# One expert's first 128 rows computed from a shorter list, between the steps of the last routing; expert weights loaded three chunks a block

## The chip, the cores and the metric

The kernel runs on one core of a Trainium2 chip. The metric is the device time of one execution in microseconds (us); a run's figure is the median of its executions.

## What is computed

One layer: an RMSNorm with modulation, a bidirectional HGRN2 mixer over 1024 latent and 256 context tokens, a residual, then a second norm and a mixture of experts (16 experts of width 256, two per token, chosen within the best group of four), a residual and a final RMSNorm. All data is float32. The part that matters here:

```python
s = jax.nn.sigmoid(h @ router_w)                    # h: (1024, 1024), 16 experts
sel = (s + router_b).reshape(n, 4, 4)
top_v, top_i = lax.top_k(sel, 2)
best = jnp.argmax(jnp.sum(top_v, axis=-1), axis=-1)
ids = best[:, None] * 4 + jnp.take_along_axis(top_i, best[:, None, None], axis=1)[:, 0]
w = jnp.take_along_axis(s, ids, axis=1); w = w / jnp.sum(w, axis=-1, keepdims=True)
for e in range(16):
    a = jax.nn.silu(h @ w_gate[e]) * (h @ w_up[e])
    y = y + combine[:, e:e + 1] * (a @ w_down[e])
```

With the given inputs expert 0 gets 140 of the 1024 tokens: 103 from the first six blocks of 128 tokens and 37 from the last two. The experts' counts are 140, 121, 148, 99, 307, 289, 122, 94, 81, 84, 119, 52, 47, 104, 143 and 98.

## The kernel before, in words

The order of instructions on every engine is the order of the code (a manual schedule), with hardware semaphores between engines. The change lies in the last third.

**The output projection and the routing** (loop `for b in range(2, NLB)` and what follows it). For each block b of 128 tokens TensorE (PE) multiplies the mixer's output with the output weights (`yo`, L904 to L906), VectorE (DVE) adds the residual (`x_evac`, `x_add`, L1012 and L1017) and forms the normed row h (`x_norm`, L1045), which SyncE (SP) stores to `h2_d` in DRAM. One block behind follow the router: `x_flip` transposes the block on PE (L1058; ScalarE (ACT) copies it, L1059), `partial` multiplies it with the router's weights (L1069), `logits` finishes that (L1076), `choose` picks the experts on DVE (L1089 to L1120), and `rank` counts on PE (L1127 to L1131, tile `pos`) which place in its expert's list each token takes, on top of `cum`, the counts of all blocks before. `enlist` (L1157) and `enlist_weights` with `enlist_rest` (L1172, L1178) write the token numbers and the weights, by one-hot matmuls that accumulate over all blocks, into the two PSUM tables `tab[0]` and `tab[1]`. Column q = 8 e + j of a table is the j-th list of 128 rows of expert e.

After the last block the tables are copied to `tidx` (L1317) and `wtab`, the counts to `cnt`. A place in a list with no token holds a number that is out of bounds, and the indirect DMAs skip it.

**Loading the experts' weights.** SP loads them in chunks of 512 KB (`load_chunk`, L962 and L965) into slots `ew`. Thirteen chunks have slots before the expert loop: experts 0 and 1's gate and up (0 to 7), expert 0's down (8, 9) and part of expert 2's. From b = 2 on, two chunks follow each block, and the thirteenth follows the loop. Each chunk is split into a high and a low float32r part: the high one on ACT (`split_hi`, L985), the low one on DVE or GpSimd (POOL) (`split_lo`, L990).

**The expert loop.** For expert e and list j: POOL gathers the 128 rows from `h2_d` (`fetch`, L1181), PE transposes them (`flip`, L1367; ACT and DVE split them, L1374 and L1375), then 24 matmuls (`gate_up`, L1381 to L1383), the activation (`act`, L1387 and L1388), two transposes (`flip_a`), 12 matmuls (`down`, L1407 to L1409), the weighting (L1410), and POOL adds the rows to `x1_d` in DRAM with an accumulating indirect DMA (`add_rows`, L1396). `finish` starts the next expert's `flip` before this expert's `down`. An expert with more than 128 rows takes a second pass (the branch `more`), one with more than 256 a third; `deep`, skipped here, does more. Ahead of the loop POOL gathers the first list of expert 0 (`gbuf[0]`) and clears two buffers (L1363), and after the branch for `deep` it gathers expert 0's second list if there is one (`fetch_if(0, 1)`), clears a buffer (L1509) and gathers expert 1's first list, then expert 2's.

## Time and profile before

| | us |
|---|---|
| median of 3 runs (lowest, highest) | 1112.74 (1108.35, 1114.17) |
| the profiled execution's own time | 1110.9 |
| span of its trace | 1108.6 |
| PE busy | 1040.0 (94%) |
| DVE busy | 695.7 (63%) |
| ACT busy | 506.8 (46%) |
| POOL busy | 260.6 (24%) |

The profile is of one execution; the times in it count from the span's start. A busy PE counts overlapping matmuls, so the spacing of their starts is what one costs. The profile's first part gives busy times by engine, its second the span in slices; the windows give the same for any stretch, with the granted clock of TensorE as a fraction of its full 2.4 GHz (0.50 is 1.2 GHz). The timelines list instructions in order with the idle time ahead of each.

### The profile page before, as it was taken

How to read it: one execution, taken by the hardware profiler on the slowest of the kernel's cores; microseconds unless marked ns; L12 is line 12 of the kernel's file. 1: busy time of each engine (PE TensorE's matmuls, PEld its weight loads, DVE VectorE, ACT ScalarE, POOL GpSimd, SP SyncE). 2: the span in 40 equal slices, each digit the busy share in tenths (PEclk: the TensorE clock that was granted, in tenths of full speed). 3: DMA queues.
4: the chain of work that ended last, by engine and by line, in shares of the span. 5: the costliest groups of instructions: out<-in, count | busy, mean ns of one | idle time of the engine just before them, and what ended most of it. 6: DMA issues, size and time to landing. Idle time of an engine off the chain costs nothing.

```text
span 1108.6 us, 16315 instructions
## 1 busy us (share of the span) xinstructions
PE 1040.0 (94%) x5847; PEld 858.9 (77%) x5847; DVE 695.7 (63%) x1339; ACT 506.8 (46%) x852; POOL 260.6 (24%) x208
## 2 busy tenths in 40 slices
PE   4988999999999999999999999989995999999986
PEld 2566888888888888889889897777774878877764
DVE  3686541146558476584745648777787665588856
ACT  4676231226436273462825635432224553377544
POOL 1353020000000000000000001531114765487834
PEclk9999999999999999999999999999995999999998
DMA  8704443421333214240120301445647997699947
GB/s 298 273 10 143 142 133 110 134 73 57 101 95 105 82 48 134 62 130 22 39 62 20 100 20 53 168 171 178 218 144 256 299 290 242 178 321 322 321 106 303
DMA packets 126225, 165.30 MB, mean 149 GB/s; under 512 B 10099, under 2 KB 93188, under 8 KB 126114
## 3 DMA queue, kind: packets, MB, share of 16 engines
q1 hardware_dynamic: 119634, 147.50, 39.8%
q0 software_dynamic: 6480, 16.39, 6.3%
q8 instruction: 61, 1.00, 0.4%
q14 instruction: 50, 0.41, 0.1%
HBM read 138.02 MB, written 33.05 MB: 154 GB/s over the span
## 4 chain that ended last, share of the span: by engine, by line
PE 64%; DMA 17%; DVE 11%; issue 3%; ACT 2%; POOL 1%; SPq 1%; POOLq 0%; DVEq 0%; ACTq 0%
PE proj L122 10%; PE proj L124 10%; PE proj L123 10%; DMA gb<-h_d,tidx 6%; PE proj L748 3%; PE proj L747 3%; PE proj L749 3%; PE sc L527 3%; DMA x_d<-y,ci 3%; PE o L553 2%; DMA ew<-in_moe_w_gate_dram 2%; PE kv L499 2%; DMA ew<-in_moe_w_up_dram 2%; DMA x_d<-y,tidx 2%; PE yo L904 2%
## 5 line engine op out<-in xcount | busy, mean ns | idle before, releaser
L122 PE MATMUL proj<-HL,whi 128*128 128x512 f32 x512 | 205.7, 402 | 1.6 <-POOL wlo L92 1.1
L123 PE MATMUL proj<-HL,whi 128*128 128x512 f32 x512 | 201.4, 393 | 6.1 <-POOL HL L298 5.5
L124 PE MATMUL proj<-HL,wlo 128*128 128x512 f32 x512 | 200.9, 392 | 1.2 <-DVE wlo L92 1.2
L560 POOL TENSOR_TENSOR oss<-oss,mhalf 128x4 f32<-128x4 f32 x16 | 16.2, 1010 | 472.1 <-DVE oss L559 472.1
L123 PEld LDWEIGHTS proj<-HL,whi 128*128 128x128 f32 x512 | 97.0, 189 | 28.0 <-POOL HL L298 8.4
L122 PEld LDWEIGHTS proj<-HL,whi 128*128 128x128 f32 x512 | 96.9, 189 | 24.1 <-issue 3.0
L124 PEld LDWEIGHTS proj<-HL,wlo 128*128 128x128 f32 x512 | 96.7, 189 | 22.1 <-DVE wlo L92 1.6
L145 ACT ACTIVATE s<-proj 128x512 f32<-128x512 f32 (+1 forms) x46 | 24.0, 523 | 182.9 <-PE proj L124 182.8
L631 DVE SCALAR_TENSOR_TENSOR macc<-mw,sc,macc 128x512 f32<-128x512 f32 x56 | 42.8, 765 | 45.2 <-DMA mw<-in_w_mod_dram 45.2
L503 DVE SCALAR_TENSOR_TENSOR w<-w,ge,kv 128x128 f32<-128x128 f32 x112 | 37.5, 347 | 40.1 <-PE kv L499 37.3
L748 PE MATMUL proj<-vl,HL 128*128 128x512 f32 x128 | 50.3, 393 | 1.2 <-DVE vl L726 1.0
L747 PE MATMUL proj<-vh,HL 128*128 128x512 f32 x128 | 50.1, 391 | 0.0
L92 DVE TENSOR_TENSOR wlo<-ws,whi 128x1024 fp32r<-128x1024 f32 (+1 forms) x31 | 37.8, 1220 | 19.4 <-ACT whi L91 19.4
L749 PE MATMUL proj<-vh,HL 128*128 128x512 f32 x128 | 49.8, 389 | 0.0
L756 ACT COPY vs<-proj 128x512 f32<-128x512 f32 x20 | 11.8, 588 | 78.5 <-PE proj L749 70.0
L1375 DVE TENSOR_TENSOR tl<-mt,th 128x512 fp32r<-128x512 f32 x46 | 29.7, 686 | 27.8 <-ACT th L1374 27.7
L553 PE MATMUL o<-w,qi 128*128 128x128 f32 x256 | 41.3, 284 | 3.6 <-DVE qi L541 1.7
L390 DVE TENSOR_TENSOR_SCAN s<-smask,s 128x1024 f32<-128x1024 bf16 x16 | 36.5, 2282 | 10.2 <-ACT s L383 10.2
L990 POOL TENSOR_TENSOR dn0l<-ew,dn0h 128x1024 fp32r<-128x1024 f32 x16 | 38.3, 2418 | 6.2 <-ACT dn0h L985 6.1
L553 PEld LDWEIGHTS o<-w,qi 128*128 128x128 f32 x256 | 35.1, 198 | 4.6 <-DVE qi L541 2.8
L1387 ACT ACTIVATE ab<-gu 128x256 f32<-128x256 f32 x23 | 8.8, 384 | 65.1 <-PE gu L1383 65.1
L558 ACT ACTIVATE jk<-o 128x128 bf16<-128x128 f32 x64 | 17.8, 277 | 43.9 <-PE o L553 42.3
(467 smaller groups left out, 2739.3 us busy)
## 6 DMA issues: line engine op xcount, KB each, us to landing
ws<-in_hg_w_in_dram SPq DMA_DIRECT2D x36, 512.0 KB, 4.6
mw<-in_w_mod_dram SPq DMA_DIRECT2D x64, 256.0 KB, 2.9
ew<-in_moe_w_gate_dram SPq DMA_DIRECT2D x64, 256.0 KB, 6.5
ew<-in_moe_w_up_dram SPq DMA_DIRECT2D x64, 256.0 KB, 7.0
ew<-in_moe_w_down_dram SPq DMA_DIRECT2D x32, 512.0 KB, 9.2
v_d<-vs SPq DMA_DIRECT2D x20, 256.0 KB, 2.2
v<-v_d SPq DMA_DIRECT2D x8, 640.0 KB, 5.9
xt<-in_x_dram SPq DMA_DIRECT2D x8, 512.0 KB, 5.4
```

What stands on the lines that cost most here:

```text
L92: (G if "l" in pool else V).tensor_sub(lo[:, o, :], ws[:, o, :], hi[:, o, :].bitcast(F32))
L122: PE.matmul(ps[:, :n], hi[:, k, :], Hhi, start=(k == 0), stop=False)
L123: PE.matmul(ps[:, :n], hi[:, k, :], Hlo, start=False, stop=False)
L124: PE.matmul(ps[:, :n], lo[:, k, :], Hhi, start=False, stop=(k == KT - 1))
L390: V.tensor_tensor_scan(L[:, rev], smask[:, 0:T], L[:, rev], 0.0, OP.mult, OP.add)
L503: V.scalar_tensor_tensor(w[:, n + 1, :], w[:, n, :], ge[:, 16 + n:17 + n], p[:, i, :], op0=OP.mult, op1=OP.add)
L553: PE.matmul(p[:, i, :], qi[d][:, i, :, :].rearrange("p j t -> p (j t)"), hd["w", d][:, lat_block(d, l), :], start=False, stop=(d == 1))
L631: V.scalar_tensor_tensor(mod_rest[r], w, sc[:, 0, k:k + 1], mod_rest[r], op0=OP.mult, op1=OP.add)
L747: PE.matmul(ps, hi, wh, start=(k == 0), stop=False)
L748: PE.matmul(ps, hi, wl, start=False, stop=False)
L749: PE.matmul(ps, lo, wh, start=False, stop=(k == KT - 1))
L990: eng.tensor_sub(gl, staged.pop(i), gh.bitcast(F32))
```

## The change

The tables are read once more, early. In the pass of the last block (b = 7), when blocks 0 to 5 are enlisted, `early_list` reads expert 0's first list from `tab[0]` and its weights from `tab[1]` (tiles `eix`, `ewt`), gathers these rows into `early["x"]`, and raises expert 0's count in `cum` to at least 128, so that expert 0's tokens of blocks 6 and 7 go to its second list. `early_flip` transposes the rows, `early_gate` multiplies one of eight row groups with the weights as loaded (plain float32, no split), and its eight calls are strewn between the steps of the last routing. The activation, two transposes and four float32 matmuls of the down projection follow, and `add_rows(ey, eix)` adds the result, all ahead of `deep`. In the expert loop expert 0 then begins with list 1 (`base(0)` is 1), held in `gbuf[0]`; its list 0 is never gathered again. Weights are loaded three chunks a block from b = 2 on, none after the loop. SP is added to the engines that get the branch hint of `deep`.

```diff
+    eix = mp.tile([128, 1], I32, name="eix")
+    ewt = mp.tile([128, 1], F32, name="ewt")
...
+    def gather_rows(dst, ix, n=T):
+        G.indirect_dma_start(out=dst, out_offset=None, in_=h2_d[0:n, :],
+                             in_offset=bass.IndirectOffsetOnAxis(ap=ix, axis=0), bounds_check=n - 1, oob_is_err=False)
...
+    early = {}
+    def early_list():
+        PE.matmul(pos[:, GB, :], onb, cum, start=True, stop=True, skip_group_check=True)
+        V.tensor_scalar(eix, tab[0][:, 0:1], pio, None, op0=OP.add)
+        early["x"] = cp.tile([128, D], F32, name="xr", bufs=2)
+        gather_rows(early["x"], eix, T - 256)
+        S.copy(ewt, tab[1][:, 0:1])
+        short = ct([1], "short")
+        V.tensor_scalar(short[0:1], pos[0:1, GB, 0:1], -1.0, float(CAP), op0=OP.mult, op1=OP.add)
+        V.scalar_tensor_tensor(cum[0:1, 0:1], short[0:1], 0.0, cum[0:1, 0:1], op0=OP.max, op1=OP.add)
+    def early_flip():
+        t_ = early["t"] = cp.tile([128, D], F32, name="x1", tag="x1", bufs=2).rearrange("p (k n) -> p k n", k=KT)
+        for hf in range(2):
+            p = yop.tile([128, 512], F32, name="yo", bufs=3).rearrange("p (k n) -> p k n", k=4)
+            for k in range(4):
+                PE.transpose(p[:, k, :], early["x"][:, (hf * 4 + k) * 128:(hf * 4 + k + 1) * 128], ident)
+            S.copy(t_[:, hf * 4:hf * 4 + 4, :], p)
+        early["p"] = yop.tile([128, 512], F32, name="yo", bufs=3)
+    def early_gate(*ks):
+        for k in ks:
+            PE.matmul(early["p"], early["t"][:, k, :], staged[k // 2][:, k % 2 * 512:k % 2 * 512 + 512], start=(k == 0),
+                      stop=(k == KT - 1))
...
         if b == NLB - 1:
+            early_list()
             choose(NLB - 2)
...
-        for i in range(2 * b - 4, 2 * b - 2):
+        for i in range(3 * b - 6, 3 * b - 3):
             if i < NC0:
                 load_chunk(i)
-    for i in range(2 * NLB - 4, NC0):
-        load_chunk(i)
     x_norm(NLB - 2)
     partial(NLB - 1, low)
+    early_flip()
     x_flip(NLB - 1, 1)
     enlist(NLB - 2)
+    early_gate(0)
     partial(NLB - 1, high)
+    early_gate(1)
     x_norm(NLB - 1, (0,))
     logits(NLB - 1)
     enlist_rest()
     x_norm(NLB - 1, (1,))
+    early_gate(2, 3, 4)
...
     choose(NLB - 1)
     rank(NLB - 1)
+    early_gate(5, 6)
     enlist(NLB - 1)
...
-    gather(gbuf[0], 0)
+    gather(gbuf[0], 1)
...
     enlist_weights(NLB - 1)
+    early_gate(7)
     enlist_rest()
+    ebuf = dn_tiles(1, F32)[1].rearrange("p k n -> p (k n)")
+    ea, eat, ey = ebuf[:, 0:DE], ebuf[:, DE:2 * DE].rearrange("p (k n) -> p k n", k=2), ebuf[:, D:2 * D]
+    S.activation(ea, early["p"][:, 0:DE], AF.Silu)
+    V.tensor_tensor(ea, ea, early["p"][:, DE:], OP.mult)
+    eap = yop.tile([128, 512], F32, name="yo", bufs=3)[:, 0:DE].rearrange("p (k n) -> p k n", k=2)
+    for k in range(2):
+        PE.transpose(eap[:, k, :], ea[:, k * 128:(k + 1) * 128], ident)
+    S.copy(eat, eap)
...
+    def base(e):
+        return 1 if e == 0 else 0
...
+    for hf in range(2):
+        o = slice(hf * 512, (hf + 1) * 512)
+        for k in range(2):
+            PE.matmul(dpp[hf], eat[:, k, :], staged[8 + k][:, o], start=(k == 0), stop=(k == 1))
+        V.scalar_tensor_tensor(ey[:, o], dpp[hf], ewt, g2r[:, o], op0=OP.mult, op1=OP.mult)
+    add_rows(ey, eix)
     deep()
...
-    fetch_if(0, 1)
     fetch_if(0, 2)
...
-    flip(0, 0)
+    flip(0, base(0))
```

In the loop `gate_up`, `act`, `finish` and `before` take `base(e)` where they had 0.

PE, from the last block's first half of the router (`partial`, low) to the branch of `deep`. Before (`ctr` is the router's work, `tab` the two tables, `pos` the counts):

```order
L1069 MATMUL ctr<-x1T,rwp 32x128 x4
L1058 MATMUL ctr<-ident,x_7036 128x128 x4
L1157 MATMUL tab_6119<-qoh,roh 128x128 x2
L1069 MATMUL ctr<-x1T,rwp 32x128 x4
L1076 MATMUL ctr<-four,lt 128x16
L1178 MATMUL tab_6120<-qow,roh 128x128 x2
...
L1131 MATMUL pos<-msk,tri 128x16
L1157 MATMUL tab_6119<-qoh,roh 128x128 x2
...
L1178 MATMUL tab_6120<-qow,roh 128x128 x2
L1472 TENSOR_LOAD cnt
```

And changed (`yo<-ident,xr` is `early_flip`, `yo<-ew` is `early_gate`, `dp<-ew` is the early down projection; four of these last, two shown):

```order
L1071 MATMUL ctr<-x1T,rwp 32x128 x4
L1208 MATMUL yo<-ident,xr 128x128 x8
L1060 MATMUL ctr<-ident,x_7044 128x128 x4
L1159 MATMUL tab_6121<-qoh,roh 128x128 x2
L1214 MATMUL yo<-ew_6049,x_7185 128x512
L1071 MATMUL ctr<-x1T,rwp 32x128 x4
L1214 MATMUL yo<-ew_6049,x_7185 128x512
L1078 MATMUL ctr<-four,lt 128x16
L1180 MATMUL tab_6122<-qow,roh 128x128 x2
L1214 MATMUL yo<-ew_6050,x_7185 128x512 x2
L1214 MATMUL yo<-ew_6051,x_7185 128x512
...
L1133 MATMUL pos<-msk,tri 128x16
```

Further down two gate matmuls stand between `pos` and `tab[0]`, one between `tab[0]` and `tab[1]`, and the two transposes and four down matmuls between `tab[1]` and the first `TENSOR_LOAD`.

POOL, from the gather of expert 0's rows to that of expert 1's. Before:

```order
L1181 DMA gb_6045<-h_d,tidx 128x1024
L1363 MEMSET gb_7309 128x1024
L1363 MEMSET gb_7311 128x1024
L1472 TENSOR_LOAD cnt
...
L1181 DMA gb_7309<-h_d,tidx 128x1024
...
L1509 MEMSET gb_7307 128x1024
L1181 DMA gb_7307<-h_d,tidx 128x1024
```

And changed:

```order
L1183 DMA gb_6047<-h_d,tidx 128x1024
L1413 MEMSET gb_7352 128x1024
L1413 MEMSET gb_7354 128x1024
L1446 DMA x_d<-dn1l,eix 1024x1024
L1522 TENSOR_LOAD cnt
...
L1564 MEMSET gb_7350 128x1024
L1183 DMA gb_7350<-h_d,tidx 128x1024
```

The accumulating DMA of the early rows now stands ahead of the branch and of expert 1's gather (`gb_7350`), and the gather of expert 0's second list (before, into `gb_7309`) is gone.

SP, the end of the last two blocks. Before and changed:

```order
L1026 DMA x_d<-x_7036 128x1024
L962 DMA ew_6057<-in_moe_w_gate_dram 128x2x256
L962 DMA ew_6057<-in_moe_w_up_dram 128x2x256
...
L1049 DMA h_d<-h_6864 128x1024
L1047 DMA h_d<-h_7042 128x512 x2
```

```order
L964 DMA ew_6061<-in_moe_w_gate_dram 128x2x256
L964 DMA ew_6061<-in_moe_w_up_dram 128x2x256
L1028 DMA x_d<-x_7044 128x1024
L1051 DMA h_d<-h_6872 128x1024
L1049 DMA h_d<-h_7050 128x512 x2
```

The last three chunks (six DMAs) no longer stand between the last block's x1 and its h rows.

## Rows read from the trace of the kernel before

**Rows 1.** Windows by stage: us, busy time per engine, PEclk, DMA share, GB/s.

```profile
840.00:850.00 10.00, 2.05 (x7) 1.64 (x7) 5.75 (x22) 3.81 (x6) 5.52 (x4) 0.50 0.58 199
...
871.00:980.00 109.00, 108.61 (x524) 88.37 (x523) 68.15 (x108) 57.40 (x85) 64.54 (x35) 1.00 0.82 243
...
980.00:1060.00 80.00, 76.07 (x359) 59.64 (x358) 68.23 (x92) 56.28 (x77) 62.12 (x31) 1.00 1.00 319
```

**Rows 2.** Timeline of PE, 832 to 853 us: start, length, instruction [idle before <-releaser].

```profile
832.45 1.08 PE L1058 MATMUL ctr<-ident,x 128*128 128x128 f32 x4 [2.55 <-DVE x L1017]
...
835.28 0.61 PE L1076 MATMUL ctr<-four,lt 128*128 128x16 f32 x2 [0.41 <-DVE lt L1072]
...
839.06 0.17 PE L1131 MATMUL pos<-msk,tri 128*128 128x16 bf16 x1 [2.10 <-DVE msk L1116]
...
841.26 0.79 PE L1157 MATMUL tab<-qoh,roh 128*128 128x128 f32 x2 [2.03 <-DVE qoh L1147]
...
844.11 1.22 PE L1178 MATMUL tab<-qow,roh 128*128 128x128 f32 x4 [2.02 <-DVE qow L1172]
...
851.19 1.94 PE L1367 MATMUL mt<-ident,gb 128*128 128x128 f32 x8 [5.86 <-DMA gb<-h_d,tidx]
...
853.01 0.80 PE L1381 MATMUL gu<-gu0h,th 128*128 128x512 f32 x1
```

**Rows 3.** Windows around TensorE's clock, columns as in rows 1.

```profile
831.50:832.00 0.50, 0.00 (x0) 0.00 (x0) 0.47 (x2) 0.00 (x0) 0.00 (x0) 0.80 0.00 0
...
855.50:856.00 0.50, 0.50 (x4) 0.37 (x3) 0.50 (x2) 0.50 (x2) 0.50 (x1) 0.80 0.98 342
```

**Rows 4.** Timeline of PE, 859 to 877 us: expert 0's second pass, expert 1.

```profile
859.92 1.03 PE L1367 MATMUL mt<-ident,gb 128*128 128x128 f32 x8
...
867.21 1.04 PE L1367 MATMUL mt<-ident,gb 128*128 128x128 f32 x8
...
871.02 0.48 PE L1381 MATMUL gu<-gu4h,th 128*128 128x512 f32 x1
...
876.70 1.04 PE L1367 MATMUL mt<-ident,gb 128*128 128x128 f32 x8
```

**Rows 5.** Timeline of DVE, 828 to 872 us.

```profile
828.18 0.16 DVE L1138 SCALAR_TENSOR_TENSOR rm<-rt,row 128x2 f32<-128x2 f32 x1
...
842.09 0.35 DVE L1317 TENSOR_SCALAR tidx<-tab,pio 128x128 int32<-128x128 f32 x1 [0.55 <-PE pos L1315]
...
843.71 0.60 DVE L1172 TENSOR_SCALAR qow<-iop,rq,wr 128x128 f32<-128x128 f32 x2
...
871.08 0.75 DVE L1410 SCALAR_TENSOR_TENSOR y<-dp,wtab,g2r 128x512 f32<-128x512 f32 x1 [0.47 <-PE dp L1409]
```

**Rows 6.** Timeline of ACT, 817 to 872 us.

```profile
817.90 1.08 ACT L1059 COPY x1T<-ctr 128x512 f32<-128x512 f32 x2 [0.86 <-PE ctr L1058]
...
833.57 0.59 ACT L1059 COPY x1T<-ctr 128x512 f32<-128x512 f32 x1 [0.45 <-PE ctr L1058]
...
871.30 0.37 ACT L1392 CAST ax0h<-sp 128x256 fp32r<-128x256 f32 x1 [2.25 <-PE sp L1367]
```

**Rows 7.** Timeline of POOL, 844 to 873 us.

```profile
844.79 2.98 POOL L1181 DMA_INDIRECT gb<-h_d,tidx  x1 [3.41 <-DVE qow L1172]
...
852.60 1.00 POOL L1181 DMA_INDIRECT gb<-h_d,tidx  x1 [2.96 <-issue]
...
854.85 1.63 POOL L1181 DMA_INDIRECT gb<-h_d,tidx  x1 [0.27 <-POOL gb L1509]
...
872.12 1.64 POOL L1396 DMA_INDIRECT x_d<-y,tidx  x1 [6.32 <-DMA gb<-h_d,tidx]
```

**Rows 8.** Tile view of the gathers that POOL starts at 854.85, 857.73, 859.89.

```profile
DMA to landing us min/median/max: 6.0/7.7/9.3
```

**Rows 9.** Chain of waits near the end: start, length, what.

```profile
1085.01 1.72 PE mt L1561 x4
```

**Rows 10.** Chain of waits, last store of the routed rows.

```profile
837.21 6.57 DMA h_d<-h
```

More of the change, by code (lines that the diff above doesn't have):

```diff
@@ L1178, in enlist_rest @@
             PE.matmul(tab[1], r_.bitcast(F32), q_, start=first, stop=last, skip_group_check=True)
+    def gather_rows(dst, ix, n=T):
+        G.indirect_dma_start(out=dst, out_offset=None, in_=h2_d[0:n, :],
+                             in_offset=bass.IndirectOffsetOnAxis(ap=ix, axis=0), bounds_check=n - 1, oob_is_err=False)
     def gather(dst, q):
-        G.indirect_dma_start(out=dst, out_offset=None, in_=h2_d,
-                             in_offset=bass.IndirectOffsetOnAxis(ap=tidx[:, q:q + 1], axis=0),
-                             bounds_check=T - 1, oob_is_err=False)
+        gather_rows(dst, tidx[:, q:q + 1])
+    early = {}
[20 more added lines that the diff above has]
+                      stop=(k == KT - 1))
     alls, low, high = range(KT), range(KT // 2), range(KT // 2, KT)
@@ L1310 @@
     tc.mark_branch_hint_location("deep", "LikelyTaken", [mybir.EngineType.PE, mybir.EngineType.Activation,
-                                                         mybir.EngineType.Pool, mybir.EngineType.DVE])
+                                                         mybir.EngineType.Pool, mybir.EngineType.DVE,
+                                                         mybir.EngineType.SP])
     choose(NLB - 1)
     rank(NLB - 1)
+    early_gate(5, 6)
     enlist(NLB - 1)
@@ L1339 @@
     NJ, NS = T // CAP, 3
+    def base(e):
+        return 1 if e == 0 else 0
     def rows_of(e, j):
-        return gbuf[(e % 3, 3 + e % 2, 5)[j]]
+        return gbuf[0 if j == base(e) == 1 else (e % 3, 3 + e % 2, 5)[j]]
     def fetch(e, j):
@@ L1446, in finish @@
             return
-        with tc.If(nval[e] > (j + 1) * CAP, label=f"more{e}" if j == 0 else None) as cmp:
+        with tc.If(nval[e] > (j + 1) * CAP, label=f"more{e}" if j == base(e) else None) as cmp:
             flip(e, j + 1)
@@ L1457, in before @@
     def before(e, j):
-        if j == 0:
+        if j == base(e):
             if e < NE - 1:
@@ L1530 @@
             split_chunk(i + 1, V)
-        tc.mark_branch_hint_location(f"more{e}", nval[e] > CAP, [mybir.EngineType.PE])
-        gate_up(e, 0)
+        tc.mark_branch_hint_location(f"more{e}", nval[e] > (base(e) + 1) * CAP, [mybir.EngineType.PE])
+        gate_up(e, base(e))
         if e + 1 < NE:
@@ L1539 @@
             fetch(e + 3, 0)
-        act(0)
+        act(base(e))
         if e + 1 < NE:
@@ L1546 @@
                 load_chunk(q + NCH)
-        finish(e, 0)
+        finish(e, base(e))
         fetch_if(e + 1, 2)
```

## The prediction

> **What bounds the kernel now.** I read the windows by stage first, then the timelines of PE and POOL over the change, then the chain of waits for single prices. From 871 to 980 us PE is busy 108.6 of 109 us, and from 980 to 1060 it is busy 95% beside a DMA share of 1.00 [rows 1]: the expert loop runs at PE's pace, its end almost so, with the weights' loads filling the DMA engines. What expert 1 gains or loses at its start is therefore carried to the end of the kernel. The stretch before is different. From 840 to 850 us PE is busy 2.05 of 10 us [rows 1]: the last routing is a chain of small steps on DVE with PE waiting 2.55, 0.41, 2.10, 2.03 and 2.02 us between them, and then 5.86 us for the gather of expert 0's rows [rows 2]. TensorE's granted clock falls to its lower level, 1.2 GHz, just before 832 us, in the first of these waits, and is back at 2.4 GHz only after 855.5 us, some 4.5 us after PE started to work without pause at 851.19 [rows 2, 3].
>
> **What is removed.** Expert 0 has 140 rows and takes two passes. The second starts at 859.92 and expert 1's 24 matmuls at 871.02, 11.1 us later [rows 4]. In the changed kernel the loop has one pass for expert 0, so this stretch shrinks to the flip of expert 1's rows: at most 1.8 us at the low clock (851.19 to 853.01 [rows 2]). **If nothing else waits, 9.3 us go.**
>
> **What is added ahead of the end of the routing.** I follow it to the table `tidx`, which DVE starts at 842.09 and ends at 842.44 [rows 5].
> - DVE: three small instructions in `early_list`. A small one costs 0.16 us, spaced by about 0.2 [rows 5]; DVE works here without a gap, so 0.65 us.
> - ACT: the two copies of `early_flip`, 1.08 us for two [rows 6], stand ahead of the copy that the last router step needs; ACT was idle for 0.45 us there [rows 6], so 0.6 us.
> - PE, `early_flip`: eight transposes, 1.03 us [rows 4], in PE's idle 2.55 us [rows 2]. They wait for the early gather. That cannot be issued before DVE has `eix`, by the order of DVE about 824.5; with 1 us of issue and 6.4 us from start to use (844.79 to 851.19 [rows 2, 7]) it is there at about 832, a little before PE's next step is due at 833.1. I take nothing; if it comes late, PE stands, in order, and every us late is a us of the chain.
> - PE, `early_gate`: a float32 matmul of 128x512 is two records; four took 1.72 us at the end of the kernel, at the high clock [rows 9], so 0.86 us each, or 1.72 at the low clock. Gate 0 lies mostly beside ACT's copies (0.3 us seen), gate 1 covers a wait of 0.41 us (0.45 us seen). Gates 2 to 4 with `tab[1]`'s matmuls (0.6 at the high clock) take 3.2 us where PE's next step was 3.17 us away (835.89 to 839.06), gates 5 and 6 1.7 us where PE waited 2.03, and gate 7 is inside 2.02 us [rows 2]: hidden. All this at the high clock. PE now works almost without pause from 832 on, so I expect the clock back by about 837, as it came back after 4.5 us of work before; the chain's own matmuls that ran at the low clock gain some tenths.
>
> Sum to `tidx`: 0.65 + 0.6 + 0.3 + 0.45 = **2.0 us later**, 844.4.
>
> The three chunks that SP issued ahead of the last h rows are loaded earlier, where there is room. The last store of h took 6.57 us, to 843.78 [rows 10], and set the time of the first gather; now it is early and `tidx` is what counts. That buys 1.3 us of the 2.0 for expert 0's gather, which is in time anyway, as the next part shows.
>
> **The new wait.** The early rows' result is added to `x1_d` by a DMA that POOL issues ahead of the branch and of the gather for expert 1, and POOL works in order. So that gather now waits for the early down projection, which has no cover:
> - DVE's `qow` ends at 844.31 [rows 5], now 846.3. Behind it: `tab[1]`'s matmuls 0.6 us (half of 1.22 at the low clock [rows 2]), two transposes 0.25 (a quarter of 1.03 [rows 4]), ACT's copy of 128x256 0.4 [rows 6], four float32 matmuls 3.44 [rows 9], the weighting 0.75 [rows 5], hand-overs 0.2: 851.9.
> - POOL's add: 0.3 to start, 1.64 [rows 7], so 853.9.
> - Branch and counter reads: POOL's gap of 2.96 us ahead of the gather at 852.60; then a clear and a gap, 1.25 us from the end of that gather to the start of expert 1's at 854.85 [rows 7]. So expert 1's gather starts at 858.1, against 854.85 now.
> - Its landing: 6.0, 7.7 and 9.3 us for this gather and the two behind it [rows 8]. I take 7.0, near its own value with a little for the add's traffic: **865.1**.
>
> Before, expert 1's rows were needed at 867.21 [rows 4] and had landed by 861. Now PE ends expert 0's single pass at about 860 (its gather at 851.8, 1.8 us of flip, 5.6 to 6.9 of matmuls) and stands still for some 5 us. In that idle time the clock falls, as it did at 832 [rows 3]. Flip 1.8 us and two transposes 0.25: expert 1 starts at 867.2, with 1.2 us to come for its first matmuls at the low clock (853.01 to 859.92 took 6.9 us, 871.02 to 876.70 5.7 [rows 2, 4]). That is 868.4 against 871.02: **2.6 us faster**, so 6.7 of the 9.3 us are lost to the new wait. The profiled execution took 1110.9, which makes 1108.3; it lies 1.8 below the median, so for the median 1112.7 - 2.6 = **1110.1**.
>
> The bounds: the landing between 6.0 and 9.3 us moves this by -1.0 and +2.3, the sum to `tidx` between 0.65 (DVE alone) and 3.0 by -1.35 and +1.0. So 2.6 lies between 5.0 faster and 0.7 slower. By the Trainium skill (DMA: Bandwidth & Descriptors, Anatomy of one DMA) a DMA from GpSimd takes about 2.0 us plus its bytes at 436 GB/s, 3.2 us for these 512 KB as an estimate; by that the gather would land 3.8 us earlier and the gain would be 6.4 us. The rows here show twice that under load.
>
> **The rivals.**
> - *The whole pass is won* (over 5.5 us). The gather for expert 1 would have to land by 860, 5 us before my figure, so that PE passes from expert 0 to expert 1 without a pause: 9.3 us, 1103.4. For it: of the 2.96 us on POOL I do not know what is left when the branch's code is ready, and the landing may be short. Against it: on POOL the add stands in front in the changed order, and 4.0 us of float32 matmuls and transposes must be done first. Chance 0.23, with all that lies between.
> - *The clock never falls.* If the transposes and gates keep TensorE at 2.4 GHz from 832 on, the chain's matmuls take half (0.8 us less over the 1.08 and 0.61 us of flip and `logits` [rows 2]), `tidx` is 1.2 us late, not 2.0, and the gain is 3.4 us: 1109.3. For it: the first idle stretch is broken up. Against it: the transposes wait for the early gather, so PE is idle for 2 us first, about as long as before the fall. Chance 0.15. The Trainium skill (TensorE: Matmul & The Clock Gate, HAM oscillation) has it that waits make the array's clock fall and unbroken work keeps it up; by that rule filling the waits is worth something, and the trace agrees that the clock fell in the first of them.
> - *The gates clog the routing* (slower). It decides if the clock is not back when gates 2 to 4 start, near 839. At the low clock gate 0 adds 0.8 and gate 1 0.85 us more, gates 2 to 4 with `tab[1]` take 6.4 us against 3.2, and gates 5 and 6 3.4 against 2.03: `tidx` is about 8 us late. The float32 matmuls behind cost another 4.3. Expert 1's gather starts near 868.7 and expert 1, by the same steps, at 879.0: 8.0 us slower, 1120.7. For it: PE has pauses at the chain's waits. Against it: from 834 on these are short. Chance 0.1.
> - *The change does not do what it says.* If early rows were still computed in the loop, no pass would go; the loop's code starts expert 0 at list 1, so I give this nothing.
>
> **How the numbers follow.** About 0.5% (5.6 us) is what a measurement of this kernel can tell from no change. My forecast, 1107.8 to 1113.4, has 0.52 and the clock's rival 0.15; both lie within it. Over 5.6 us faster: 0.23 from the first rival and 0.02 from the early ends of the forecast, 0.25. Slower by over 5.6: 0.1 from the clogged routing. That leaves 0.65 for the same. The range takes in the forecast with its bounds, most of the first rival and the start of the third: 1102.5 to 1118.0.
>
> **What would show it.** Right: 22 passes through the experts' activation, not 23; POOL's add of the early rows near 852, its gather for expert 1 near 858; PE idle some 5 us before expert 1's flip, that wait ended by a gather, the clock low again after it; `tidx` about 2 us later. Wrong: expert 1 starting before 862 or after 873, the early transposes held up past 834 by their gather, or gates at 1.72 us after 840.

## The result: 6 to 7 us slower, and the profile after

| | before | after |
|---|---|---|
| median of 16 runs each, same chip (us) | 1111.55 | 1118.57 |
| ratio, with its 95% interval | 1 | 1.0056 [1.0033, 1.0078] |
| the profiled execution's own time | 1110.9 | 1121.3 |
| span of its trace | 1108.6 | 1119.5 |

The change costs 7.0 us by the medians. The execution that was profiled shows 10.4 us, for single executions of the changed kernel lie between 1113.57 and 1123.06; the two traces say where. Expert 0 does run one pass less, and PE is busy for longer all the same:

```profile
PE 1046.6 (93%) x5836; PEld 859.7 (77%) x5836; DVE 691.7 (62%) x1339; ACT 506.2 (45%) x853; POOL 257.2 (23%) x208
```

The windows of the changed kernel, with the stages of [rows 1] and one more ahead of them (columns as there: length, busy time of PE, PEld, DVE, ACT and POOL, PEclk, DMA share, GB/s), and the additional window in the kernel before:

```profile
820.00:840.00 20.00, 18.11 (x117) 12.21 (x106) 17.71 (x72) 7.93 (x16) 3.60 (x5) 1.00 0.28 101
840.00:850.00 10.00, 6.45 (x17) 3.19 (x16) 7.56 (x22) 4.36 (x8) 3.69 (x4) 0.75 0.52 146
871.00:980.00 109.00, 105.31 (x500) 85.58 (x501) 66.86 (x103) 54.06 (x81) 64.66 (x35) 0.99 0.83 254
980.00:1060.00 80.00, 72.18 (x330) 58.08 (x328) 56.81 (x84) 51.81 (x70) 54.09 (x27) 0.95 0.99 319
```

```profile
820.00:840.00 20.00, 13.82 (x97) 10.48 (x95) 17.78 (x72) 6.91 (x13) 2.83 (x5) 0.80 0.42 138
```

Two things are new. Up to 840 us TensorE's waits in the routing are mostly filled and its clock is granted at 2.4 GHz throughout (1.00; it was 0.80 before in the same window). And in the expert loop, which the prediction took as fixed, PE is idle for 3.7 us up to 980 and 7.8 us up to 1060; before it was 0.4 and 3.9 [rows 1].

**The routing and the start of expert 1.** The timeline of PE, changed kernel, against [rows 2, 4]:

```profile
831.91 0.63 PE L1060 MATMUL ctr<-ident,x 128*128 128x128 f32 x4 [1.48 <-DVE x L1019]
...
836.14 2.74 PE L1214 MATMUL yo<-ew,x 128*128 128x512 f32 x6
...
845.63 1.22 PE L1180 MATMUL tab<-qow,roh 128*128 128x128 f32 x4 [2.85 <-DVE qow L1174]
...
847.74 5.67 PE L1555 MATMUL dp<-ew,dn1l 128*128 128x512 f32 x8 [0.46 <-ACT dn1l L1370]
854.58 1.06 PE L1417 MATMUL mt<-ident,gb 128*128 128x128 f32 x8 [1.16 <-PEq L1479]
...
868.63 1.94 PE L1417 MATMUL mt<-ident,gb 128*128 128x128 f32 x8 [6.58 <-DMA gb<-h_d,tidx]
...
871.41 0.77 PE L1431 MATMUL gu<-gu4h,th 128*128 128x512 f32 x1 [0.41 <-DVE tl L1425]
```

The gates (`yo<-ew`) run in the waits at the high clock: three of them (x6) in 2.74 us. `tidx` starts at 841.83 on DVE, against 842.09 [rows 5]. The changed kernel came to the last block 0.54 us ahead (DVE's residual of its second half, `x_add`, starts at 831.07, before 831.61), so the routing lost 0.3 us. From there on the time runs away: DVE's two one-hot products of the last weights, 0.60 us before [rows 5], take 2.19, PE waits 2.85 us for them, the early down projection follows partly at the low clock (5.67 us), and expert 1's flip then waits 6.58 us for its rows. Its first matmul starts at 871.41; before, with two passes of expert 0 ahead of it, at 871.02 [rows 4]. The whole 9.3 us of the removed pass are gone at this point.

DVE and POOL of the changed kernel in the same stretch (timelines); the POOL rows answer to [rows 7]:

```profile
841.83 0.35 DVE L1354 TENSOR_SCALAR tidx<-tab,pio 128x128 int32<-128x128 f32 x1 [0.41 <-PE pos L1352]
...
843.45 2.19 DVE L1174 TENSOR_SCALAR qow<-iop,rq,wr 128x128 f32<-128x128 f32 x2
```

```profile
842.47 1.15 POOL L1183 DMA_INDIRECT gb<-h_d,tidx  x1 [1.21 <-DVE most L1358]
843.63 1.86 POOL L1413 MEMSET gb<- 128x1024 f32 x2
854.49 1.63 POOL L1446 DMA_INDIRECT x_d<-dn1l,eix  x1 [9.00 <-DVE dn1l L1556]
861.90 0.95 POOL L1564 MEMSET gb<- 128x1024 f32 x1 [5.78 <-remote]
863.12 1.34 POOL L1183 DMA_INDIRECT gb<-h_d,tidx  x1 [0.27 <-POOL gb L1564]
```

The long `qow` lies beside POOL's clearing of two buffers (843.63 to 845.49), which before came 4 us behind it. And POOL stands still for 5.78 us between its scatter-add of the early rows and its next instruction; expert 1's gather starts at 863.12, 8.63 us behind the start of the add. Where it stands is in the view of one line, L1523, the branch `deep` (min, median and longest of its semaphore waits in ns):

```profile
L1523 POOLq EVENT_SEMAPHORE  x5: 17/42/4973, 855.3 to 860.6; - x5
```

The hold reaches ACT too. Its first split of expert 1's weights waits, as built, for the same eight semaphores of POOL's DMAs; it starts only when POOL is through:

```profile
861.22 1.05 ACT L987 CAST gu4h<-ew 128x1024 fp32r<-128x1024 f32 x1 [4.85 <-remote]
```

Behind it, in order, come DVE's low parts and then expert 0's activation (`ab`, DVE, 865.71 to 866.13), which PE needs ahead of expert 1's first matmul. So rows that landed earlier would not have started expert 1 before about 866.

**The expert loop.** From the flip at 877.46 (before 876.70) to that at 973.56 (before 972.55) the changed kernel goes from 0.8 to 1.0 us behind. This last flip stands in expert 6's step, and I call it expert 6's, though the rows are those of expert 7: behind the jump for an expert of one pass (the short path) come the next expert's flip and the last one's down projection. Behind it the changed kernel has four stalls, all at the same place of the code, in the down projection of the steps of experts 6, 8, 10 and 12 (PE timeline):

```profile
977.97 0.56 PE L1457 MATMUL dp<-dn1h,ax1h 128*128 128x512 f32 x1 [2.67 <-issue]
...
1001.60 0.39 PE L1457 MATMUL dp<-dn1h,ax1h 128*128 128x512 f32 x1 [2.86 <-issue]
...
1024.70 0.40 PE L1457 MATMUL dp<-dn1h,ax1h 128*128 128x512 f32 x1 [2.33 <-issue]
...
1048.14 0.39 PE L1457 MATMUL dp<-dn1h,ax1h 128*128 128x512 f32 x1 [2.63 <-issue]
```

"issue" says that nothing the profile shows holds them, and the fourth matmul of a down projection waits for no semaphore. Three of the stalls let the granted clock fall as well (0.56, 0.62 and 0.93 in the 1.1 to 1.4 us behind the first three). The view of the DMA queues has something to offer: between 974.9 and 976.7 us, in the first stall, one packet of an instruction queue starts, and one in each of the other three (packets, MB, share of the 16 engines):

```profile
q8 instruction: 1, 0.02, 3.6%
```

The Trainium skill (Runtime: NRT & Kernel Launch, Instruction fetch mechanics) says that an engine's program is fetched in blocks of 16 KiB, 256 instructions, and that a jump into a block that is not there holds the engine until it is fetched. The trace agrees so far: 16 KB in one packet, and PE works again at 977.97, 1.3 us behind the end of its record (975.64 to 976.67). From expert 6's flip to that of expert 14's second pass (1075.12, before 1064.56) the changed kernel takes 101.6 us, the kernel before 92.0.

### The profile page after: what moved, and what is told of

It reads as the page before. It is cut to its first block, busy times and chain, and to the rows that moved or that the text cites. A ratio compares the mean times of both kernels' runs of the same rounds, so it can differ in the third digit from the quotient of the medians.

```text
span 1119.5 us, 16259 instructions
## 1 busy us (share of the span) xinstructions
PE 1046.6 (93%) x5836; PEld 859.7 (77%) x5836; DVE 691.7 (62%) x1339; ACT 506.2 (45%) x853; POOL 257.2 (23%) x208
## 4 chain that ended last, share of the span: by engine, by line
PE 77%; DVE 10%; DMA 6%; issue 3%; ACT 2%; POOL 1%; SPq 1%; POOLq 0%; DVEq 0%; another core or an unknown queue 0%; ACTq 0%
PE proj L122 10%; PE proj L124 10%; PE proj L123 10%; PE gu L1431 3%; DMA xr<-h_d,eix 3%; PE gu L1432 3%; PE proj L748 3%; PE gu L1433 3%; PE proj L747 3%; PE proj L749 3%; PE sc L527 3%; PE o L553 2%; PE kv L499 2%; PE dp L1457 2%; PE dp L1458 2%
## 5 line engine op out<-in xcount | busy, mean ns | idle before, releaser
L122 PE MATMUL proj<-HC,whi 128*128 128x256 f32 (+1 forms) x128 | 37.1, 290 | 0.0
```

Source lines behind the costliest of these rows:

```text
L122: PE.matmul(ps[:, :n], hi[:, k, :], Hhi, start=(k == 0), stop=False)
```

## The experiments

My theories: (a) **landing**: POOL's branch waits until its own outstanding indirect DMAs have landed; (b) **placement**: the four stalls come from where the experts' code lies in blocks of the program, which every added or removed instruction ahead of it moves; (c) **contention**: POOL beside VectorE makes some of VectorE's operations several times as long. The rivals were the counters and the branch itself for (a), the weights' transfers for (b), late inputs for (c). In the table "start" is the time from DVE's `tidx` to expert 1's first matmul, "stretch" that from expert 6's flip to expert 14's second, both from the profiled execution; ratios are to the kernel before on the same chip (its medians there: 1111.55 to 1114.89).

| run | median us | ratio [95%] | start | stretch |
|---|---|---|---|---|
| before | | 1 | 28.9 | 92.0 |
| after | 1118.57 | 1.0056 [1.0033, 1.0078] | 29.6 | 101.6 |
| pad72 | 1116.70 | 1.0031 [1.0004, 1.0058] | 28.8 | 100.6 |
| before_pad184 | 1116.06 | 1.0028 [1.0001, 1.0055] | 29.6 | 98.6 |
| late_add | 1116.17 | 1.0029 [0.9998, 1.0059] | 26.2 | 99.4 |
| late_pad72 | 1114.75 | 1.0000 [0.9972, 1.0028] | 26.6 | 100.0 |
| pad40 | 1113.22 | 0.9991 [0.9966, 1.0016] | 28.3 | 91.0 |
| before_pad224 | 1109.40 | 0.9969 [0.9945, 0.9993] | 29.1 | 91.5 |
| late_sep | 1110.67 | 0.9974 [0.9947, 1.0000] | 18.0 | 98.1 |
| late_sep_pad40 | 1104.70 | 0.9919 [0.9892, 0.9947] | 18.0 | 94.2 |
| gather_behind | 1108.21 (one execution) | | 23.0 | 96.3 |
| late_sep_pad88 | 1107.73 | 0.9952 [0.9921, 0.9982] | 18.0 | 96.3 |
| sep_only | 1118.15 | 1.0056 [1.0029, 1.0083] | 29.3 | 98.4 |

### pad72: dead code that moves the experts' code

```diff
+                            if e == 0 and j == NS:
+                                turn(mtp[1], g_[:, 512:1024], 4)
-                            for k in range(KT):
+                            for k in list(range(KT)) * (3 if e == 0 and j == NS else 1):
                                 PE.matmul(gup[0], thf[:, k, :], gu[k // 2][:, k % 2, :], ...)
```

This is inside `deep`, in the branch that no execution enters here.

> The changed kernel with 72 more TensorE instructions in a branch that is never taken (the one for experts with more than 384 rows), ahead of all experts; the work done is the same. Theory, placement: the four stalls of 2.3 to 2.9 us in the down projections of experts 6, 8, 10 and 12 are waits for a 16 KB block of TensorE's program, which falls due 25 instructions behind the jump into the short path; the added instructions put the experts' code where it lay in the kernel before. Then no stall of over 1.5 us is left there, the stretch from the flip of expert 6 (973.56) to that of expert 14's second pass (1075.12) goes from 101.6 us to about the 92.0 us of the kernel before, and the profiled time from 1121.3 to about 1112. Rival, traffic: the stalls come from the weights' transfers, which fill the DMA engines from 970 us on (share 0.90 to 1.05), whatever the place of the code: the four stalls stay and the time stays at about 1118 to 1121.

The four stalls are gone. But two others stand in their place, at the flip itself, the first instruction behind the jump, in experts 8 and 12 (PE timeline):

```profile
996.61 1.94 PE L1417 MATMUL mt<-ident,gb 128*128 128x128 f32 x8 [4.64 <-issue]
...
1042.77 1.94 PE L1417 MATMUL mt<-ident,gb 128*128 128x128 f32 x8 [4.98 <-issue]
```

So placement is right about the four stalls, and wrong in what it promised: the stretch is 100.6 us, not 92, and the median 1116.70. The rival falls as the cause of the four, since no transfer of weights was touched. The kernel before, whose experts lie at the same instructions of a block, has one of the two, and small:

```profile
992.73 1.06 PE L1367 MATMUL mt<-ident,gb 128*128 128x128 f32 x8 [0.88 <-issue]
```

Its instruction packet starts at 990.05, 1.8 us before PE has come to the end of the work ahead of the jump (991.85); in pad72 it starts at 993.93, 2.0 us after (991.97). So the place in a block does not settle alone what a jump costs; what calls the packet earlier in one kernel is not shown.

### before_pad184: the stalls in the kernel before

The same edit in the kernel before, 184 instructions (five more repeats of the eight matmuls, three of `turn`).

> The kernel before with 184 more TensorE instructions in the same never taken branch, which put the experts' code where it lies in the changed kernel. Placement: four stalls of 2 to 3 us appear behind the jump into the short path of experts 6, 8, 10 and 12, with none of the change in the kernel, and the profiled time goes from 1110.9 to 1117 to 1121 (the stalls give back some of the waits for weights that this stretch has now). Rival, traffic: nothing but the never taken code differs, so the trace and the time stay as they are, 1111.

```profile
975.99 0.50 PE L1407 MATMUL dp<-dn1h,ax1h 128*128 128x512 f32 x1 [2.86 <-issue]
...
997.95 0.57 PE L1407 MATMUL dp<-dn1h,ax1h 128*128 128x512 f32 x1 [2.60 <-issue]
...
1020.69 0.49 PE L1407 MATMUL dp<-dn1h,ax1h 128*128 128x512 f32 x1 [1.87 <-issue]
...
1042.89 0.50 PE L1407 MATMUL dp<-dn1h,ax1h 128*128 128x512 f32 x1 [1.31 <-issue]
```

The PE timeline has the four stalls, at the same matmul of the same four experts, in a kernel that has nothing of the change. The time rises by 0.28%, 3 us, less than expected. This shows (b) for the four stalls, and that they cost the kernel before about half of what the change does. The program explains the pattern: as built, the code of one expert is 384 PE instructions (marks of jump targets left out), one and a half times 256, so every second expert meets a block's edge at the same instruction. In the changed kernel the even experts' short path begins some 25 instructions ahead of an edge, enough for 1.7 us of PE's work (973.56 to 975.30); that of the odd ones begins some 150 ahead of it and shows nothing.

### pad40 and before_pad224: a better place for both

> The changed kernel with 40 more TensorE instructions in the never taken branch. With 72 more, the four stalls of 2.6 us were gone and two of 4.6 and 5.0 us stood in their place, at the jumps into the short path of experts 8 and 12: there the jump comes some 20 instructions behind the end of a 16 KB block and goes into a block that is not there. Theory, placement: with 40 more, gate, jump and the end of a block lie so that every short path is entered in the block right behind the one that holds the jump, with over 200 instructions left in it. Then experts 6 to 13 show no stall of over 1 us behind issue, and the stretch from expert 6's flip to expert 14's second is 86 to 92 us (101.6 in the changed kernel, 92.0 in the kernel before; 9 passes at 9.52 us are 85.7): profiled time 1105 to 1112. Rival: the blocks can't be fetched in time whatever the place while the weights fill the DMA engines; stalls of 10 us in all appear elsewhere and the time stays at 1116 to 1120.

> The kernel before with 224 more TensorE instructions in its never taken branch: the experts' code lies as in the run with 40 more in the changed kernel, so that the two can be compared with the place of the code taken out. Placement: its one stall of 0.88 us behind issue goes, the waits for weights among experts 6 to 13 stay: same as the kernel before or up to 6 us less, 1105 to 1111. Rival: nothing moves, 1111 to 1115.

Both as expected, though pad40 only just: its stretch of 91.0 us and its profiled time of 1111.57 are near the slow end of what was given. What is left there behind issue is 0.43 and 0.40 us at two flips, and waits for weights have come back that the stalls had covered, as in the second row from its PE timeline:

```profile
993.36 1.07 PE L1417 MATMUL mt<-ident,gb 128*128 128x128 f32 x8 [0.40 <-issue]
...
1043.09 0.50 PE L1432 MATMUL gu<-gu6l,th 128*128 128x512 f32 x1 [1.42 <-DVE gu6l L992]
```

The place of the code is worth 1.0056 - 0.9991 = 0.65% (7 us) in the changed kernel and 0.31% (3.4 us) in the kernel before. With both in this better place the change stands at 0.9991 against 0.9969, 2.4 us slower, and the intervals overlap. The other two pairs whose experts lie alike point the same way: pad72 is at 1.0031 of the kernel before, and the changed kernel at 1.0056 against 1.0028 of before_pad184. So with the place taken out the change seems to cost 0.22 to 0.31%, 2.4 to 3.4 us of the 7; no pair alone is clear enough to show it (pad72's interval, [1.0004, 1.0058], only just misses 1). That it gains, as forecast, none of them says.

### late_add: the scatter-add behind the gathers

```diff
-    ea, eat, ey = ..., ebuf[:, D:2 * D]
+    ea, eat = ...
+    ey = ybuf[1]
...
-    add_rows(ey, eix)
     deep()
...
     for i in (1, 2):
         G.memset(gbuf[i], 0.0)
         fetch(i, 0)
+    add_rows(ey, eix)
```

> The changed kernel with the early pass's scatter-add of expert 0 issued behind the gathers of experts 1 and 2 instead of ahead of the branch on the largest count; its rows stand in an output buffer for that. Theory, landing: GpSimd's branch waits until its own outstanding indirect DMAs have landed; without the add ahead of it, it waits for the gather of 842.5 alone, and expert 1's gather is issued at about 852 (863.12 now) and lands at about 858. Expert 1's flip then follows expert 0's pass at about 862 and its first matmul starts at 864 to 866 (871.41 now); 5 to 7 us earlier from there on, with the four stalls as they are. Rival, counters: the 6 us are the read of the counts and the branch themselves, whatever stands ahead of them: the gather stays at about 862 to 863 and the time at 1118 to 1121. Rival, weights: the gather goes early, but the experts from 6 on are paced by the weights' transfers and the 6 us are lost again before 1060.

```profile
L1523 POOLq EVENT_SEMAPHORE  x5: 17/43/2812, 842.2 to 842.6; - x5
```

```profile
846.60 0.95 POOL L1564 MEMSET gb<- 128x1024 f32 x1 [2.87 <-remote]
847.82 1.00 POOL L1183 DMA_INDIRECT gb<-h_d,tidx  x1 [0.27 <-POOL gb L1564]
...
857.31 5.71 POOL L992 TENSOR_TENSOR dn0l<-ew,dn0h 128x1024 fp32r<-128x1024 f32 x2
```

Landing holds: with only the gather on its way, POOL's hold at the branch (view of its line) shrinks from 4.97 to 2.81 us, and the POOL timeline has expert 1's gather at 847.82, 15 us earlier. Expert 1 gains 3.3 us of start, not 5 to 7: its flip no longer waits for rows, but POOL, set free early, now runs `dn0l` beside DVE's subtractions, and PE waits for DVE (timelines of PE and DVE):

```profile
865.62 0.69 PE L1417 MATMUL sp<-ident,ab 128*128 128x128 f32 x2 [4.67 <-DVE ab L1438]
```

```profile
857.40 3.42 DVE L992 TENSOR_TENSOR gu4l<-ew,gu4h 128x1024 fp32r<-128x1024 f32 x1
860.74 3.36 DVE L992 TENSOR_TENSOR gu5l<-ew,gu5h 128x1024 fp32r<-128x1024 f32 x1
864.02 1.21 DVE L992 TENSOR_TENSOR gu6l<-ew,gu6h 128x1024 fp32r<-128x1024 f32 x1
```

The same subtraction takes 3.4 us beside POOL's `dn0l` and 1.21 behind it. It looks like a second case of what `qow` did beside POOL's clears; late_sep tests both.

### late_pad72: both edits

> Both edits together. Placement and landing together: 1112 less 5 to 7 us, 1105 to 1107. If the weights' transfers pace experts 6 to 13 (the kernel before has 6 us of small waits there with the DMA engines' share at 1.02 to 1.07), the 5 to 7 us are eaten between 970 and 1060 and the time stays at 1110 to 1112.

1114.75 us, and 1.0000 of the kernel before: the late add again gives 0.3%, but neither sum was met, because pad72's place has the two jumps that miss (4.10 and 5.11 us in this run). It says nothing on the weights.

### late_sep: POOL kept off VectorE, with the late add

```diff
-    for i in (3, 5):
-        G.memset(gbuf[i], 0.0)
...
     count(0)
+    G.memset(gbuf[5], 0.0)
     fetch_if(0, 2)
...
-    G.memset(gbuf[4], 0.0)
+    for i in (4, 3):
+        G.memset(gbuf[i], 0.0)
...
-        if e + 1 < NE:
+        if e + 1 < NE and e:
             for q in (i + 4, i + 5):
...
         finish(e, base(e))
+        if e == 0:
+            for q in (i + 4, i + 5):
+                split_lo(q, V)
+                load_chunk(q + NCH)
```

> The kernel with the late scatter-add, and besides GpSimd kept off three VectorE operations that took two to four times as long beside it: the zeroing of two gather buffers is moved from beside the two one-hot products of the last weights (2.19 us for both beside it, 0.60 in the kernel before) to behind the branch, and expert 0's two low parts of down weights go from GpSimd (beside them two of expert 1's splits took 3.42 and 3.36 us, 1.21 elsewhere) to VectorE behind expert 0's pass. Theory, contention: the products take 0.6 us, TensorE's wait of 2.85 us falls to about 1.3, expert 0's activation is multiplied at about 861 instead of 865.2 and expert 1's first matmul starts 3 to 6 us earlier than with the late add alone (866.31), at 861 to 863; the four stalls of the experts' code stay. 1116 less 3 to 6: 1110 to 1113. Rival, order: those operations were long because their inputs came late, and moving GpSimd's work changes nothing: 1116.

```profile
843.25 0.60 DVE L1174 TENSOR_SCALAR qow<-iop,rq,wr 128x128 f32<-128x128 f32 x2
```

```profile
843.65 0.75 PE L1180 MATMUL tab<-qow,roh 128*128 128x128 f32 x4 [1.07 <-DVE qow L1174]
...
845.14 3.70 PE L1554 MATMUL dp<-ew,dn1l 128*128 128x512 f32 x8 [0.46 <-ACT dn1l L1370]
...
859.61 0.47 PE L1429 MATMUL gu<-gu4h,th 128*128 128x512 f32 x1 [0.49 <-ACT ax0h L1440]
...
904.96 0.50 PE L1430 MATMUL gu<-gu5l,th 128*128 128x512 f32 x1 [2.38 <-DVE gu5l L992]
```

Contention, and more than expected: `qow` is back at 0.60 us, and the PE timeline has expert 1's first matmul at 859.61. The start is 18.0 us, 8.3 less than with the late add alone and 10.9 less than in the kernel before. Not all of it reaches the end: expert 4 now waits 2.38 us for its weights' low part, so that from `tidx` to expert 6's flip 8.5 us are left of the 11.6 won on the changed kernel. The Trainium skill (SBUF — State Buffer, SBUF: two separate sides) has VectorE and GpSimd share a pair of ports that one of them holds for a whole instruction while the other stands. The trace agrees: two short products stretch to the length of two clears, 2.19 against 1.86 us.

### sep_only: the same without the late add

> The changed kernel with GpSimd kept off VectorE alone: the scatter-add stays ahead of the branch, the code lies as badly as in the changed kernel. Contention: the wait for the last weights' products falls from 2.85 to 1.1 us and the early pass's down projection, at full clock, ends 3 to 4 us earlier; the add, and with it expert 1's gather, its flip and its first matmul, follow 3 to 4 us earlier too (867.5 to 868.5, 871.41 now): 1118.6 less 3 to 4, 1114 to 1116. If the late add is what makes the room, expert 1's start does not move by over 1 us and the time stays at 1117 to 1119.

```profile
849.88 1.63 POOL L1444 DMA_INDIRECT x_d<-dn1l,eix  x1 [6.48 <-DVE dn1l L1554]
858.31 0.95 POOL L1560 MEMSET gb<- 128x1024 f32 x1 [6.81 <-POOLq L1477]
859.20 0.95 POOL L1563 MEMSET gb<- 128x1024 f32 x1
860.43 1.75 POOL L1183 DMA_INDIRECT gb<-h_d,tidx  x1 [0.27 <-POOL gb L1563]
```

A miss, and a telling one: the add goes out 4.6 us earlier and the start is 29.3 us, as in the changed kernel. Three things use the gain up. POOL is held longer (8.4 us from the add to its next instruction, 7.4 in the changed kernel); the edit itself puts a second clear ahead of expert 1's gather, 0.9 us; and the gather takes 7.7 us to the flip, 5.5 in the changed kernel. So the late add alone won 3.3 us of start, POOL kept off VectorE alone 0.3, and both 11.6: each loss hid behind the other. Why the add and the gather landed later here is not shown.

### gather_behind: nothing on its way at the branch

In late_sep's kernel, `gather(gbuf[0], 1)` moved from ahead of the counts to right behind `deep()`.

> The kernel of the run with the late add and GpSimd kept off VectorE, with the gather of expert 0's second list column issued behind GpSimd's branch on the largest count instead of ahead of it, so that nothing of GpSimd's is on its way when it comes to the branch. In that run GpSimd comes to the branch at about 842 (the gather of 840 to 841.5 is its last instruction) and its next instruction starts some 6 us later. Theory, landing: the branch waits for the gather to land; without it, GpSimd's first instruction behind the branch starts 1 to 3 us after the largest count is made, at 842 to 844. Rival, counters: reading the count and the branch take the 6 us, so that the first instruction stays at 846 to 848. The time is not asked for: expert 0's own rows come later.

```profile
L1520 POOLq EVENT_SEMAPHORE  x5: 17/43/43, 842.4 to 842.8; - x5
...
L1520 POOLq INC_SWDGE_SEM  x1: 207/207/207, 842.9 to 842.9; - x1
```

```profile
844.06 2.41 POOL L1183 DMA_INDIRECT gb<-h_d,tidx  x1 [3.98 <-DVE dn1l L1365]
```

The hold is gone: the longest of the branch's five semaphore waits is 0.043 us, against 3.34 in late_sep, 4.97 in the changed kernel and 6.15 in sep_only. The last of them starts at 842.8. POOL's first instruction came at 844.06, at the end of what landing gave and 2 us ahead of what the counters gave. The built program's order on POOL names the cause; the row of the skipped side, from the changed kernel (in brackets what a row waits for, DMASW0 to 7 being the queues of POOL's own DMAs):

```
L1523 ISA [waits Pool_sequencer_49,DMASW4_49,DMASW5_49,DMASW3_49,DMASW6_49,DMASW2_49,DMASW7_49,DMASW1_49,DMASW0_49]
```

The branch's body holds DMAs of all eight queues. The side that skips it brings the eight semaphores to the count that the body would have left (INC_SWDGE_SEM), and for that it must wait for whatever is on its way on any of them. The first seven queues of the row wait in the EVENT_SEMAPHOREs, the last, DMASW0, on INC_SWDGE_SEM itself, so that a hold can stand in either row. In the kernel before it stands in the second: the one gather ahead of its branch is on DMASW0, no EVENT_SEMAPHORE lasts over 0.043 us, and the view of the branch (L1473) has

```profile
L1473 POOLq EVENT_SEMAPHORE  x5: 17/43/43, 845.9 to 846.2; - x5
...
L1473 POOLq INC_SWDGE_SEM  x1: 203/203/203, 851.1 to 851.1; - x1
```

5 us after the last wait, when the gather of 844.79 had landed (6.3 us from its start in its tile view, 851.09). In gather_behind the two are 0.1 us apart. It isn't the branch that costs most; it is what was sent off ahead of it.

### late_sep_pad40 and late_sep_pad88: all three edits

> Late add, GpSimd kept off VectorE, and 40 more dead instructions: all three losses taken out. If they add up: 1118.6 less about 3 (late add), 3 to 6 (contention) and 3 to 10 (placement): 1101 to 1109, under the kernel before (1111 to 1115). If the weights' transfers pace experts 6 to 13, what comes early is lost there and the time stays at 1108 to 1112.

> The run with all three losses taken out, with 88 dead TensorE instructions for 40: the last stall of its stretch (3.86 us at the jump of expert 10) stood where the jump's target lies 10 instructions into a block. With 88, the short paths of the even experts begin 58 instructions into a block and those of the odd ones 186, with some 70 left. If the stall goes and none comes: 1104.7 less up to 4, 1100 to 1104. If a jump into a block other than the next is what costs (two stalls of 4.6 and 5.0 us at 47 instructions into a block in the run with 72): 1105 to 1110.

late_sep_pad40 takes 0.9919 of the kernel before [0.9892, 0.9947], some 8 to 9 us less, and 0.9919/1.0056 = 0.986 of the changed kernel. Against the kernel before in its better place, before_pad224 on the same chip, it is 4.7 us less (1104.70 and 1109.40); that is the fairer figure for what the early rows are worth without the losses. Its start is 18.0 us and its one large stall is a jump that misses, in expert 10:

```profile
1003.87 1.94 PE L1415 MATMUL mt<-ident,gb 128*128 128x128 f32 x8 [3.86 <-issue]
```

late_sep_pad88 was to take that away. It did, and got one of 5.54 us at expert 12 (1027.36), with waits of 0.5 us for weights in between: 0.9952. Which of two neighbouring places loses a jump is not something that I can work out from these runs.

## Why the prediction was wrong

The forecast was 1110.1, 2.6 us faster; it came out 7.0 slower by the medians and 10.4 by the profiled execution. Point by point:

- **"What expert 1 gains or loses at its start is therefore carried to the end of the kernel"** is the step that failed first. It held to expert 6 (0.4 us later at the first matmul, 1.0 later at expert 6's flip) and then, in the profiled executions, 9.6 us came from the stretch of 92.0, which the change does not touch in what it computes. before_pad184 shows the four stalls without the change, pad40 shows the loss gone with it: the code of the experts had been moved against the blocks in which TensorE's program is fetched. By the medians this is worth 0.28% (before_pad184), 3 us of the 7.0, to 0.65% (the changed kernel against pad40), 7 us. I read the diff for what it does on PE, and nothing in it looked like a cost in a loop that it leaves alone.
- **"Branch and counter reads: POOL's gap of 2.96 us"** is the second step that failed; with the next point it is why expert 1 started no earlier. It was the wrong name for a row that I had read [rows 7]. POOL came to that branch at 845.4 and went on when the gather of 844.79 had landed at 851.09; the first half of the gap (849.64, the end of the clears, to 851.09) was a landing, seen from behind, and only 1.5 us the rest. The add takes the gather's place ahead of the branch and starts late, so its landing counts in full: from the add's start to the gather's 8.63 us, where my steps have 5.9. With the early down projection 2.3 us later than I had it, the rows landed at 868.49 and not at 865.1: 3.4 of the 4.2 us by which the first matmul (871.41) missed my 867.2; the rest lies behind the landing, in two transposes of 0.63 us for my 0.25 and a wait of 0.41 us for DVE's `tl`. late_add and gather_behind show it; the waits stood in the built program's order.
- **The early down projection** was costed at 3.44 us and the high clock, behind a `qow` of 0.60. `qow` took 2.19 beside POOL's clears, PE's wait of 2.85 us let the clock fall again (0.75 in 840 to 850), and the eight records took 5.67. In late_sep, with the clears moved, they take 3.70.
- **`tidx` 2.0 us later**: it was 0.3 us earlier. The last block had a head start of 0.54 us, of unknown origin; the gates, the flip and the small instructions on DVE cost the routing 0.3 us.
- **The rivals.** *The clock never falls* came true up to 842 (granted clock 1.00 from 831 to 842, before 0.54); by the Trainium skill (TensorE: Matmul & The Clock Gate, HAM oscillation) filled waits keep it up, and the trace agrees. It fell in the next long wait. *The gates clog the routing*: no gate took 1.72 us. It named the right side and not the cause. *The whole pass is won* needed expert 1's rows by 860; late_sep shows that it can be had, and more (10.9 us), once the add is out of the way and POOL is kept off VectorE. The estimate of 3.2 us for the gather by the Trainium skill (DMA: Bandwidth & Descriptors, Anatomy of one DMA) does not fit: it took 5.37 us from its start to its landing, nearer the 6.0 to 9.3 of [rows 8].
- What held: one pass less, PE idle for 6.58 us ahead of expert 1's flip with a gather ending the wait, and the clock low behind it.

What stays open: why the jumps of experts 8 and 12 miss in pad72 and those of 6 and 10, which lie the same in a block, do not, and why the kernel before, which lies there too, hardly loses by them; when a block is called for, and which one gives way; and what the 2.4 to 3.4 us are made of that the change seems to cost at the same place of the code. Pads of 40 and 88 were tried for it, and no rule came out.

## What to carry to other kernels

A branch whose body holds DMAs can be a wait, on the side that skips the body, for every DMA that is on its way on the body's queues: send off ahead of it only what is needed right behind it, and look into the built order for what the skipped side waits for. A change of a few instructions in one place can move a loop elsewhere against the blocks in which the program is fetched; before believing a difference of half a per cent, move the code by some dead instructions, in both kernels, and compare them at their best. And when an engine is given work in a gap, look at what the others do in that gap: here VectorE and GpSimd, both at work on on-chip memory, held each other up.

## What the runs showed of the hardware

- Program code came in packets of 16 KB, one at a time. The stalls that went with it were 0.9 to 3.7 us behind 25 instructions of cover (2.3 to 2.9 in the changed kernel, 1.3 to 2.9 in before_pad184) and, at a jump's target, 3.9 to 5.5 us, or 0.4 to 0.9 where the packet had started before TensorE came to the jump. Nothing names it in the list of waits but "issue"; the row of the instruction queue (q8) shows it.
- VectorE's fp32 subtraction of two tiles in on-chip memory took 3.4 us beside GpSimd's, 1.21 to 1.23 alone, and GpSimd's pair 5.71 us, 4.73 and 4.76 in the kernels after and before; a one-hot product on VectorE 1.1 us beside a clear, 0.3 alone.
- The scatter-add of one list held POOL's branch for 4.97 us (the changed kernel) and 6.15 us (sep_only); a gather alone for 2.8 to 3.4, and for 4.9 in the kernel before; with nothing on its way no wait was over 0.043 us.
